# Adding two columns on VectorE ahead of one bfloat16 product with ones

## The chip, the core and the metric

The kernel runs on one core of a Trainium2 chip. A core has five engines that run their own lists of instructions in order and meet at semaphores: TensorE (PE in the profile; its weight loads are shown apart as PEld), VectorE (DVE), ScalarE (ACT), GpSimd (POOL) and SyncE (SP), which issues most of the transfers. The metric is the device time of one execution in microseconds, as the median of several runs.

## The reference

A transformer block over 2048 tokens of width 1024: a mixer of four HGRN2 heads and four retention heads in both directions, with a context of 256 tokens as initial state, and then a feed-forward part with a gated convolution. Cut to the parts that use the weights which matter here:

```python
hx = _rmsnorm(x, norm1_g[layer]) * (1.0 + sc1) + sh1
feats_x = _mixer_features(hx, w_in[layer], lb, (rows, cols))
...
x = x + g1 * (mix_x.astype(x.dtype) @ w_out[layer])
hx2 = _rmsnorm(x, norm2_g[layer]) * (1.0 + sc2) + sh2
gate, up = jnp.split(hx2 @ w_up_l, 2, axis=-1)
x = x + g2 * ((silu(conv(gate)) * up) @ w_down_l)
return _rmsnorm(x, final_g)
```

## The kernel before

All large products are float32 products made of float16 parts. A weight block is scaled by a power of two, split into a float16 and a float16 remainder, and multiplied in three products (`mm3`, lines 81 to 86). On top of that the projections use a seven-product block scheme: two weight tiles of 128 columns become a pair, from which seven combinations are made (`pair_blocks`, lines 638 to 646).

**The scale.** It comes from the sum of squares of the whole weight tile. ACT squares the tile, [128, 1024], and accumulates along the row, which leaves one float32 number in each of 128 partitions, a column of `ssq` (line 687 for the heads, `w_in`; line 1477 for the up projection, `w_up`). A pair of tiles gives two columns. `allsum` (lines 102 to 108) adds them over the partitions and hands the total to all of them: it multiplies a 128x128 matrix of ones (`onesq`, a view of one column with step 0) with each column, and lets the products add up in PSUM. DVE reads the total in `pow2` (lines 88 to 100), which makes the scale and its inverse by operations on exponent bits; `scales` (lines 648 to 660) adds the negative scale and the factor by which results are divided. With the scale known, ACT and DVE make the float16 parts of the weights (lines 643 and 644).

**Who calls it.** `head_weights` prepares the weights of the eight heads, always ahead of their use: per head a pair `z` and a pair `vg` (the last head has `v` and `g` as single tiles), and for the first four heads a single `q`. That gives 15 sums of two columns and 6 of one. `up_weights` is called 22 times, twice for each of the 11 blocks of the up projection, always with two columns; there, 16 small bfloat16 products (line 1482, `col`) with a column of bfloat16 ones, `onesb`, run just ahead of `allsum`. `out_weights`, `mixed_pairs` and `modulation` call it with one column, 13 times. So 37 sums have two columns and 19 have one.

**What sets the order.** The program is written as operations on tiles. A planner lays them out at build time with a simulated clock: for each engine it takes, among the instructions whose inputs are there, the one written earliest, and so it can issue an instruction well ahead of its place in the text. The order that comes out is fixed; on the chip an engine that has to wait holds up all that stands behind it in its list. Transfers of weights (`raw`, `wur`) are issued by SP. In the up projection four kinds of work share the time: PE multiplies the features by block j (lines 84 to 86), ACT and DVE take the results out of PSUM and do the convolution (lines 544 to 581), the weights of block j+1 are prepared, and the outputs of block j are split for the down projection (lines 1591 to 1593).

Of the kernel before, what the change touches and what calls it, by code (L numbers as in the profile page):

```python
# [11 lines left out]
BF16 = mybir.dt.bfloat16  # L12
# [3 lines left out]
ALU = mybir.AluOpType  # L16
PSUM = bass.MemoryType.PSUM

P = 128
# [27 lines left out]
def view(t, off, dims):  # L47
    return bass.AP(t.tensor, t.offset + off, [t.ap[0]] + dims)


class Kern:
# [49 lines left out]

    def allsum(self, cols, tag="tu"):

        o = self.ps(tag, [P, 1], "allsum")
        n = cols.shape[-1]
        for i in range(n):
            self.nc.tensor.matmul(o, self.onesq, cols[:, i:i + 1], start=i == 0, stop=i == n - 1, skip_group_check=True)
        return o

    def allmax(self, col, tag="tu"):  # L110
# [10 lines left out]
    def setup(self):  # L121

        nc, tc, ctx, I = self.nc, self.tc, self.ctx, self.I
# [19 lines left out]
        self.ones = cp.tile([P, 1], F32, name="ones")  # L143
        nc.gpsimd.memset(self.ones, 1.0)
        self.onesq = view(self.ones, 0, [[0, P]])
        self.dqx = cp.tile([P, 2], F32, name="dqx")
        self.xx = cp.tile([P, 1], F32, name="xx")
        self.sv = cp.tile([P, NV], F32, name="sv")
# [1291 lines left out]

    def ffn_setup(self):
        nc, cp = self.nc, self.cp
        self.onesb = cp.tile([P, 1], BF16, name="onesb")
        nc.vector.tensor_copy(self.onesb, self.ones)

        self.a2, self.c2 = (self.sv[:, V_BM + i * NF:V_BM + (i + 1) * NF] for i in range(2))
        t = self.slot_tile([P, 3 * NF], F32, "FG", "tabs")
        w = self.cw[:, :3 * NF]
        nc.vector.scalar_tensor_tensor(t, w, -1.0, w, ALU.mult, ALU.max)
        nc.vector.tensor_tensor(self.a2, t[:, :NF], t[:, NF:2 * NF], ALU.add)  # L1450
        nc.vector.tensor_tensor(self.a2, self.a2, t[:, 2 * NF:], ALU.add)
        nc.vector.tensor_tensor(self.a2, self.a2, self.a2, ALU.mult)
        nc.vector.tensor_scalar(self.a2, self.a2, self.xx, 2.0, ALU.mult, ALU.mult)
        c = self.cw[:, 3 * NF:]
        nc.vector.scalar_tensor_tensor(self.c2, c, 2.0, c, ALU.mult, ALU.mult)

        m = self.modT[:, 1]
        self.sas, self.ias = m[:, :NJ], m[:, NJ:2 * NJ]
        self.wq = m[:, 2 * NJ:4 * NJ], self.sv[:, :2 * NJ]
        self.W = {}  # L1460
        self.rows = {}
# [374 lines left out]
```

## Time and profile before

| what | value |
|---|---|
| median of 3 runs | 2742.63 us (2736.52 to 2743.33) |
| profiled execution | 2745.74 us |
| its span, first to last instruction | 2743.7 us |
| mean granted clock of TensorE | 0.967 |
| instructions | 56410 |

In the stretches of the span: the head weights and the first feature blocks up to about 210 us, the eight heads up to about 1230 us, the output projection up to about 1430 us, the up projection up to about 2290 us, and the down projection up to the end. Rows of the profile give the line of the kernel, the engine, the operation, what it writes and reads (`allsum<-ssqw,ones`), the shape, and how often. A timeline row begins with the start in us from the span's start and the duration; in brackets stands the idle time of the engine ahead of it, with the instruction that ended it. A group's row gives busy us and the mean ns of one. A float32 product shows as two records, each with a weight load of its own. The duration of a PE record contains the passage through the array, which overlaps with the next one's, so the start of the next record says how long PE was held. ACT's accumulated sum is read out by a second, short record (ACTIVATION_READ_ACCUMULATOR).

### The profile page before, as it was taken

Reading aid. Unit: us, or ns where it says so; the run is one execution under the profiler, and the core shown is the slowest. Engines: PE = TensorE matmul, PEld = TensorE weight load, DVE = VectorE, ACT = ScalarE, POOL = GpSimd, SP = SyncE. Lnnn points to the kernel's source line nnn. Section 1 sums busy time; section 2 is a strip of 40 time slices with the busy share of each in tenths; the row PEclk is TensorE's granted clock in tenths of the full one; section 3 lists DMA queues with packets and bytes.
Section 4 is the critical chain, followed back from the end, with each engine's and each line's share of the span. In section 5 each row is a group of like instructions: output and inputs, shape, how many; then the busy total and the mean of one; then the engine's idle time right before and its main releaser. Section 6 shows DMA issues by size and latency. Waiting matters only on the chain.

```text
span 2743.7 us, 56410 instructions
## 1 busy us (share of the span) xinstructions
PE 2562.4 (93%) x22829; PEld 1692.0 (62%) x22829; DVE 1835.8 (67%) x3569; ACT 1343.5 (49%) x2902; POOL 773.9 (28%) x905
## 2 busy tenths in 40 slices
PE   5789998999998989898999899999999999999998
PEld 2678887889888888787445344444444444444443
DVE  4998676775856666547464888778877777423553
ACT  5776456564544434336354665555555554411220
POOL 3742111220312132121244344344434433000101
PEclk7899999999999999999999999999999999999999
DMA  8224333343447766666532132333233234734552
GB/s 294 102 86 155 123 103 121 101 129 109 148 159 224 227 212 204 215 181 219 194 110 78 50 123 100 112 115 101 99 115 103 98 110 161 272 144 169 207 192 100
DMA packets 216693, 402.37 MB, mean 147 GB/s; under 512 B 16623, under 2 KB 98771, under 8 KB 211824
## 3 DMA queue, kind: packets, MB, share of 16 engines
q1 hardware_dynamic: 203808, 373.42, 40.1%
q10 hardware_dynamic: 12320, 25.18, 3.1%
q8 instruction: 178, 2.92, 0.4%
q14 instruction: 83, 0.68, 0.1%
q0 software_dynamic: 304, 0.17, 0.0%
HBM read 298.57 MB, written 91.75 MB: 142 GB/s over the span
## 4 chain that ended last, share of the span: by engine, by line
PE 63%; DVE 17%; DMA 7%; issue 6%; ACT 4%; POOL 3%; ACTq 0%; DVEq 0%; SPq 0%; POOLq 0%
PE pa L84 7%; PE pa L85 7%; PE pa L86 7%; PE pd L84 5%; PE pd L86 5%; PE pd L85 5%; PE pc L84 3%; PE pc L85 3%; PE pc L86 3%; PE pb L84 2%; PE pb L86 2%; PE pb L85 2%; PE opp L85 2%; PE opp L84 2%; PE opp L86 2%
## 5 line engine op out<-in xcount | busy, mean ns | idle before, releaser
L84 PE MATMUL pa<-feat,w 128*128 128x512 f16 x704 | 267.7, 380 | 8.6 <-ACT ta L544 8.0
L85 PE MATMUL pa<-feat,w 128*128 128x512 f16 x704 | 267.3, 380 | 1.1 <-DVE feat L1367 1.1
L86 PE MATMUL pa<-feat,w 128*128 128x512 f16 x704 | 263.9, 380 | 0.0
L85 PE MATMUL pd<-wd,actl 128*128 128x512 f16 x616 | 233.3, 379 | 0.0
L86 PE MATMUL pd<-wd,actl 128*128 128x512 f16 x616 | 233.3, 379 | 0.0
L84 PE MATMUL pd<-wd,actl 128*128 128x512 f16 x616 | 232.6, 379 | 0.1
L85 PEld LDWEIGHTS <-w 128*128 128x128 f16 x1232 | 120.8, 98 | 152.7 <-issue 12.9
L86 PEld LDWEIGHTS <-w 128*128 128x128 f16 x1232 | 121.4, 99 | 149.1 <-DVE w L644 2.9
L84 PEld LDWEIGHTS <-w 128*128 128x128 f16 x1232 | 121.7, 99 | 140.8 <-issue 1.6
L85 PEld LDWEIGHTS <-hx 128*128 128x128 f16 x1824 | 184.6, 101 | 11.7 <-issue 9.7
L86 PEld LDWEIGHTS <-hx 128*128 128x128 f16 x1824 | 184.6, 101 | 3.0 <-issue 1.9
L84 PEld LDWEIGHTS <-hx 128*128 128x128 f16 x1824 | 184.6, 101 | 2.4
L1592 DVE SCALAR_TENSOR_TENSOR st<-act,modT,st 128x512 f16<-128x512 f32 x154 | 142.9, 957 | 31.6 <-ACT st L1591 30.7
L84 PE MATMUL pa<-w_vg,hx 128*128 128x128 f16 x800 | 148.2, 224 | 5.5 <-DVE cb L578 4.6
L86 PE MATMUL pa<-w_vg,hx 128*128 128x128 f16 x800 | 148.2, 225 | 0.0
L85 PE MATMUL pa<-w_vg,hx 128*128 128x128 f16 x800 | 148.2, 224 | 0.0
L1591 ACT ACTIVATE st<-act,modT 128x512 f16<-128x512 f32 x154 | 107.5, 718 | 80.9 <-DVE act L1581 29.3
L86 PE MATMUL pc<-feat,w 128*128 128x512 f16 x352 | 134.1, 381 | 2.4 <-DVE w L644 2.4
L84 PE MATMUL pc<-feat,w 128*128 128x512 f16 x352 | 133.9, 380 | 2.3 <-ACT feat L1366 1.3
L85 PE MATMUL pc<-feat,w 128*128 128x512 f16 x352 | 133.9, 380 | 0.0
L84 PE MATMUL pa<-hx,w_z 128*128 128x256 f16 x464 | 128.7, 277 | 4.6 <-DVE K L586 2.1
L85 PEld LDWEIGHTS <-w_z 128*128 128x128 f16 x1072 | 108.7, 101 | 34.9 <-issue 23.0
(550 smaller groups left out, 7576.4 us busy)
## 6 DMA issues: line engine op xcount, KB each, us to landing
hx<-hxd SPq DMA_DIRECT2D x212, 512.0 KB, 5.0
actd<-st SPq DMA_DIRECT2D x154, 256.0 KB, 2.0
actl<-actd SPq DMA_DIRECT2D x28, 1024.0 KB, 5.1
wur<-in_w_up_dram SPq DMA_DIRECT2D x44, 512.0 KB, 4.1
raw<-in_w_in_dram SPq DMA_DIRECT2D x36, 512.0 KB, 4.3
wm<-in_w_mod_dram SPq DMA_DIRECT2D x64, 256.0 KB, 4.7
hxd<-hx SPq DMA_DIRECT2D x28, 512.0 KB, 3.4
wdb<-in_w_down_dram SPq DMA_DIRECT2D x44, 256.0 KB, 4.0
```

The source lines that it names most:

```text
L84: mm(ps, lhs(0), rhs(0), start=start, stop=False, skip_group_check=True)
L85: mm(ps, lhs(0), rhs(1), start=False, stop=False, skip_group_check=True)
L86: mm(ps, lhs(1), rhs(0), start=False, stop=stop, skip_group_check=True)
L1591: nc.scalar.activation(p[:, 0], v, AF.Copy, scale=s)
L1592: nc.vector.scalar_tensor_tensor(p[:, 1], v, s, p[:, 0], ALU.mult, ALU.subtract)
```

## The change

`allsum` with two columns now adds them on VectorE first, into a bfloat16 column `both` (two buffers), and makes one product with bfloat16 ones. With one column it does what it did: one float32 product. The bfloat16 column of ones `onesb`, so far made in `ffn_setup` by a conversion of the float32 column, is filled by a memset in `setup`. The total is thus rounded to bfloat16 per partition ahead of the sum over the partitions.

```diff
     def allsum(self, cols, tag="tu"):
 
+
         o = self.ps(tag, [P, 1], "allsum")
-        n = cols.shape[-1]
-        for i in range(n):
-            self.nc.tensor.matmul(o, self.onesq, cols[:, i:i + 1], start=i == 0, stop=i == n - 1, skip_group_check=True)
+        ones = self.onesq
+        if cols.shape[-1] == 2:
+            both = self.wp.tile([P, 1], BF16, tag="both", bufs=2, name="both")
+            self.nc.vector.tensor_tensor(both, cols[:, 0:1], cols[:, 1:2], ALU.add)
+            cols, ones = both, view(self.onesb, 0, [[0, P]])
+        self.nc.tensor.matmul(o, ones, cols, start=True, stop=True, skip_group_check=True)
         return o
...
         self.onesq = view(self.ones, 0, [[0, P]])
+        self.onesb = cp.tile([P, 1], BF16, name="onesb")
+        nc.vector.memset(self.onesb, 1.0)
...
     def ffn_setup(self):
         nc, cp = self.nc, self.cp
-        self.onesb = cp.tile([P, 1], BF16, name="onesb")
-        nc.vector.tensor_copy(self.onesb, self.ones)
```

## The prediction

> **What bounds the kernel now.** I read the page's busy shares and chain first, then the busy times by stretch, then every place where the changed sum runs.
>
> ```profile
> PE 2562.4 (93%) x22829; PEld 1692.0 (62%) x22829; DVE 1835.8 (67%) x3569; ACT 1343.5 (49%) x2902; POOL 773.9 (28%) x905
> ...
> PE 63%; DVE 17%; DMA 7%; issue 6%; ACT 4%; POOL 3%; ACTq 0%; DVEq 0%; SPq 0%; POOLq 0%
> ```
>
> TensorE (PE) is busy 93% of the span and carries 63% of the chain that ended last. A share of 93% is an average, so the stretches come next (columns: stretch, its length, then busy us and instructions of each engine in the order PE, PEld, DVE, ACT, POOL).
>
> ```profile
> 60.00:210.00 150.00, 118.46 (x1602) 101.27 (x1602) 137.82 (x295) 110.36 (x287) 87.70 (x115) 0.87 0.30 111
> 210.00:1230.00 1020.00, 936.27 (x13407) 858.52 (x13405) 674.55 (x1444) 504.10 (x1255) 208.22 (x241) 0.96 0.50 161
> ...
> 1640.00:2290.00 650.00, 648.44 (x3276) 301.81 (x3274) 521.44 (x892) 375.97 (x657) 263.64 (x175) 1.00 0.32 107
> 1430.00:1640.00 210.00, 196.67 (x1004) 94.35 (x1003) 156.95 (x264) 120.71 (x222) 94.25 (x105) 0.98 0.23 80
> ```
>
> Three regimes. From 60 to 210 us VectorE (DVE) is the fullest engine, 137.82 of 150 us. From 210 to 1230 us (heads 0 to 7) PE is busy 936.27 of 1020 us, so 83.7 us of idle time lie there. From 1640 to 2290 us (the up projection) PE idles 1.6 us in 650: whatever PE no longer issues there shortens the run one for one.
>
> **What the sum costs on PE today.** Each of the 37 two-column sums is four PE records, two per float32 column.
>
> ```profile
> L107 PE MATMUL allsum<-ssqw,ones x160: 169/250/373, 38.5 to 2272.9; 128*128 128x1 f32 x160
> ```
>
> 160 is 37 x 4 plus 6 one-column sums x 2. The 250 ns are no price: matmuls overlap, so I take start to start (the timeline of PE). First the last sum of the up projection, then two of the heads.
>
> ```profile
> 2272.43 0.29 PE L1482 MATMUL col<-onesb,w 128*128 128x1 bf16 x6
> 2272.59 0.58 PE L107 MATMUL allsum<-ssqw,ones 128*128 128x1 f32 x4
> 2273.03 0.38 PE L84 MATMUL pc<-feat,w 128*128 128x512 f16 x1
> ```
>
> ```profile
> 357.14 0.50 PE L107 MATMUL allsum<-ssqw,ones 128*128 128x1 f32 x4
> 357.51 0.27 PE L84 MATMUL pb<-hx,w_q 128*128 128x256 f16 x1
> ...
> 575.08 0.33 PE L107 MATMUL allsum<-ssqw,ones 128*128 128x1 f32 x2
> 575.28 0.36 PE L900 MATMUL o<-Sf,qf 128*128 128x128 f32 x1
> ```
>
> In the up projection the four hold PE from 2272.59 to 2273.03: **0.44 us**. In the heads, four together hold it 0.37 us, and where the planner put the two columns apart, 0.20 us per column. The replacement is one bfloat16 product with a 128x128 weight load and one moving column. That form stands just ahead: six L1482 products in 2272.43 to 2272.59, weight loads included, **0.027 us** each.
>
> Two rules of the Trainium skill would give other sums. "FP8 and Floating Point Precision", section TensorE Precision Notes, says true float32 takes four passes through the array; at 0.027 us a pass a pair would cost 0.22 us, and the 37 would save an estimated 7 us. The trace disagrees: a pair holds PE 0.44 us. "TensorE: Matmul & The Clock Gate", section LDWEIGHTS, gives a load of 128 columns as P/1.2, 107 ns, which would make the new product four times as dear and the saving an estimated 3 us smaller. The trace disagrees here too: the six loads and products came 27 ns apart.
>
> **The change, part by part.** (1) *PE, up projection.* 22 sums lie from 1430 to 2290 us. Each loses 0.44 - 0.027 = 0.41 us: 9.1 us. 17 of them lie in the stretch where PE never idles: 7.0 us, all of it on the path. Five lie from 1430 to 1640 us, where PE idles 13.3 us; of their 2.1 us I count 1.6.
>
> (2) *PE, heads.* 13 sums lie from 210 to 1230 us: five as four together, 5 x 0.37 = 1.9 us, eight in two halves, 8 x 0.40 = 3.2 us. Less 13 x 0.027 us this is 4.7 us of PE time. PE is 92% busy here, but its gaps are chains through DVE and ScalarE (ACT), some of which start at a DMA and absorb what PE saves. I take two thirds, 3.1 us; the bounds are 0 and 4.7. The two sums of head 0 stand before 210 us, where PE is not the bound: nothing.
>
> (3) *DVE, 37 adds.* The nearest form, a 128x1 add of two float32 columns:
>
> ```profile
> L1499 DVE TENSOR_TENSOR q<-q 128x1 f32<-128x1 f32 x11 | 1.7, 157 | 0.0
> ```
>
> 37 x 0.157 = 5.8 us of DVE. From 210 us on it is hidden behind PE: in the fullest stretch DVE works 521.44 of 650 us, and 17 adds are 2.7 us. If the cover were gone, all 5.8 us. One or two adds fall into the stretch from 60 to 210 us, where DVE is the bound: 0.2 us on the path.
>
> (4) *The wait.* The PE product waited for ACT's squares; now it waits for DVE, and DVE for the squares. In twelve of the 22 up sums there is ample time: the square was read out at 2247.85, its sum started at 2272.59. The other ten are tight (the first row is of the ample case, the next two of a tight one; timeline of ACT, then of DVE and PE).
>
> ```profile
> 2247.66 0.19 ACT L1477 ACTIVATION_READ_ACCUMULATOR w<-wur 128x1 f32 x1
> ...
> 2219.90 1.06 ACT L1477 ACTIVATE w<-wur 128x1024 bf16<-128x1024 f32 x1
> 2220.86 0.19 ACT L1477 ACTIVATION_READ_ACCUMULATOR w<-wur 128x1 f32 x1
> ```
>
> ```profile
> 2220.03 0.69 DVE L578 TENSOR_TENSOR ta<-pc,ta 128x512 f32<-128x512 f32 x1 [2.63 <-ACT ta L544]
> 2222.26 0.75 DVE L1561 SCALAR_TENSOR_TENSOR act<-ta,taps,act 128x511 f32<-128x511 f32 x1 [1.55 <-ACT act L1556]
> 2222.93 0.21 DVE L1567 SCALAR_TENSOR_TENSOR act<-edge,taps,act 128x1 f32<-128x1 f32 x1
> 2223.06 0.74 DVE L1562 SCALAR_TENSOR_TENSOR act<-ta,taps,act 128x511 f32<-128x511 f32 x1
> ...
> 2222.96 0.58 PE L107 MATMUL allsum<-ssqw,ones 128*128 128x1 f32 x4
> ```
>
> The squares are complete at 2221.05 and PE wants the sum at 2222.96; the add needs 0.16 us, and DVE stands idle for 1.55 us before L1561. In that hole it is done by about 2221.3. What queues behind it on DVE is L1561, which waits for ACT anyway. So I cost the wait at 0. Issued behind the three DVE rows it would delay PE by about 1 us: rival C. For the other sums, and those of the heads, the planner can move a ready instruction forward, as it did with the cast of the ones:
>
> ```profile
> L1444 DVE CAST onesb<-ones x1: 98/98/98, 1.0 to 1.0; 128x1 bf16<-128x1 f32 x1
> ```
>
> (5) *The ones.* That cast, written in the third stage, already ran at 1.0 us. A memset in its place, written in the setup, costs and saves nothing within 0.1 us. The two columns of `both` can hold up an add only until the second-last product has been read: nothing. No DMA is added or moved.
>
> **The sum.** 7.0 + 1.6 + 3.1 - 0.2 = 11.5 us less. The profiled execution took 2745.7 us (span 2743.7), so it becomes 2734.2. That execution lies 3.1 us above the median of the three runs, 2742.6; against the median the forecast is **2731 us**, 0.42% less. Below 0.3%, 8.2 us, a measurement of this kernel can't tell a change from none (its three runs lie 6.8 us apart).
>
> **Rivals.**
>
> *A, the heads give nothing* (2734): their 83.7 us of idle take up the 4.7 us. For: of the waits on the way some end at a DMA. Against: PE is busy 92%. Left is 7.0 + 1.6 us, 8.6, at the edge of what can be measured.
>
> *B, the ones are not cheap* (2734): a weight load that reads one column 128 times might take the pitch of one float32 record, 0.11 us (0.44/4). Then 35 sums save 0.085 us less each, 3.0 us. For: no row shows such a load in bfloat16. Against: two float32 loads of that one column took 0.30 us, two of a full matrix the same.
>
> ```profile
> 575.03 0.30 PEld L107 LDWEIGHTS allsum<-ssqw,ones 128*128 128x128 f32 x2
> 575.25 0.30 PEld L900 LDWEIGHTS o<-Sf,qf 128*128 128x128 f32 x2
> ```
>
> Cheaper ends than 0.027 us are worth below 1 us. By the LDWEIGHTS rule of the Trainium skill ("TensorE: Matmul & The Clock Gate") this rival would be the forecast; the 27 ns of the traced loads speak against it.
>
> *C, PE waits for the add in the tight places* (2741): if the add is issued behind the three DVE rows shown, it ends at about 2223.96 and PE waits 1.0 us. Ten such places take back 10 us of the 11.5. For: DVE is 80% busy there. Against: the hole of 1.55 us.
>
> *D, the planner's new order costs the heads something* (2742): one product fewer and one add more shift every later choice. If PE's idle time in the heads grows by an eighth, 10.5 us, the gain is gone; a better order could as well give some microseconds.
>
> *E, slower: DVE is held by late weights* (2762).
>
> ```profile
>   DMA raw<-in_w_in_dram: 29.5, 17
> ...
>   DMA wur<-in_w_up_dram: 32.5, 31
> ```
>
> These rows say how long ACT idled ahead of the squares, for `raw` (L687) and for `wur` (L1477): 62 us in all. Today only ACT is held. An add issued directly behind the square makes DVE wait as long, and with it the evacuations for which PE waits. About half, 31 us, lies ahead of the second square, which the add needs; passed on to PE in full it makes 31 - 11.5 = 19.5 us more. It decides the sign once PE is made to wait over 11.5 us. For: both engines run their lists in order. Against: DVE has other work in its list ahead of the add, and such a delay of ACT costs PE little today, as its 1.6 us of idle in 650 show.
>
> **How the numbers follow.** The forecast 0.52; A 0.11; B 0.05; C 0.10; D 0.11; E 0.11. A and B lie at the bound and count half as faster. Faster: 0.52 + 0.08 = 0.60; slower: E, 0.11; same: the rest, 0.29. For the range: all 13.8 us of (1) and (2) on the path give 2729, and a planner's order that by luck gives 4 us more, with a median run as low as the lowest of the three, 6 us, some 2719. Upward it takes in A, B, C and D and the spread of the runs above D: 2746. Left out are E and a little of the low end.
>
> **What would show it.** In the changed profile the two-column sums are 37 bfloat16 products and float32 records of `ssqw` fall from 160 to 12; PE's count falls by 111 to about 22718, DVE's grows by 37 to about 3606, and PE's busy time falls by some 14 us. From such a sum to the next product's start it is 0.03 us, not 0.44 (0.11 is B). Rows of PE waiting for the add, `both`, above 2 us in all would be C; DVE waiting for L687 or L1477 above 10 us would be E. The stretch of the up projection shortens by about 9 us; if the heads shorten by 0 it is A, if they grow it is D. I am wrong in the mechanism if PE's work falls by 14 us and the idle time of the up projection takes it back.

## The result, and the profile after

The changed kernel takes **2761.5 us** (median of 4 runs, 2756.0 to 2762.7) against 2743.0 for the kernel before (4 runs, 2736.5 to 2744.8): ratio **1.0065**, 95% interval 1.0051 to 1.0079. It is slower by 18 us where 12 us less were forecast.

What the change says it does, it does. The page's busy shares and the sum's own groups, after:

```profile
PE 2556.0 (93%) x22718; PEld 1678.2 (61%) x22718; DVE 1831.5 (66%) x3606; ACT 1342.5 (49%) x2903; POOL 777.2 (28%) x905
```

```profile
L111 PE MATMUL allsum<-both,onesb x37: 163/164/167, 38.7 to 2290.2; 128*128 128x1 bf16 x37
...
L111 PE MATMUL allsum<-ssqw,ones x12: 168/250/373, 44.5 to 1155.5; 128*128 128x1 f32 x12
```

```profile
2290.08 0.29 PE L1486 MATMUL col<-onesb,w 128*128 128x1 bf16 x6
2290.24 0.16 PE L111 MATMUL allsum<-both,onesb 128*128 128x1 bf16 x1
2290.26 0.38 PE L84 MATMUL pa<-feat,w 128*128 128x512 f16 x1
```

PE's records fell by 111 to 22718, and from the sum to the next product it is 0.02 us (the last rows, of PE's timeline) where it was 0.44. The work is gone. PE's busy time, though, fell by 6.4 us and not by the 14 that were expected: the mean granted clock of TensorE was 0.962 to 0.963 in the four runs, against 0.967 in the profiled run of the kernel before. The question is where the run got longer. I cut both spans at the same instructions: the first product `ub<-V,KTt`, the first `opp`, the first `pa<-feat,w`, the first `pd`. That gives five stages: the start, the heads, the output projection, the up projection and the down projection. Busy times by stretch, the kernel before:

```profile
0.00:183.40 183.40, 129.24 (x1324) 96.53 (x1324) 136.69 (x318) 119.87 (x301) 94.21 (x129) 0.80 0.50 180
183.40:1304.60 1121.20, 1021.25 (x14576) 937.44 (x14575) 755.53 (x1660) 568.93 (x1414) 237.90 (x288) 0.96 0.50 161
...
1492.90:2333.60 840.70, 825.81 (x4153) 384.34 (x4152) 674.51 (x1155) 486.11 (x853) 334.89 (x229) 0.99 0.32 108
```

And the changed kernel:

```profile
0.00:189.70 189.70, 129.79 (x1318) 95.87 (x1319) 137.60 (x320) 120.30 (x301) 92.68 (x129) 0.79 0.48 174
189.70:1331.50 1141.80, 1022.34 (x14537) 934.56 (x14536) 747.68 (x1673) 570.86 (x1415) 243.45 (x288) 0.96 0.49 158
...
1519.00:2350.90 831.90, 818.53 (x4091) 375.25 (x4090) 678.72 (x1177) 482.86 (x853) 335.02 (x229) 0.99 0.32 109
```

The up projection became 8.8 us shorter. The start became 6.3 us longer and the heads 20.6 us longer; the two other stages stayed within 1 us. In the heads PE was busy as long as before (1022.3 against 1021.3 us) and idle for 19.5 us more.

The first suspect is the new add. Its group on DVE, with the idle time ahead of it and what ended that:

```profile
L109 DVE TENSOR_TENSOR both<-ssqw 128x1 bf16<-128x1 f32 x37 | 14.8, 400 | 66.6 <-ACT w L1481 40.1 <-ACT w_z L693 16.4 <-ACT w_vg L693 10.1
```

DVE did stand in front of the adds for 66.6 us, 26.5 of them in the heads (L693). The figure is close to the loss, which makes it tempting. But 40.1 us lie in the up projection, the stage that won. The second suspect is the order: PE's list differs from that of before from 84 us on. Two theories follow, **HELD** (the wait of DVE is the loss) and **ORDER** (the new order is).

### The profile page after: what moved, and what is told of

It reads as the page before. It is cut to its first block, busy times and chain, and to the rows that moved or that the text cites. A ratio compares the mean times of both kernels' runs of the same rounds, so it can differ in the third digit from the quotient of the medians.

```text
span 2760.9 us, 56237 instructions
## 1 busy us (share of the span) xinstructions
PE 2556.0 (93%) x22718; PEld 1678.2 (61%) x22718; DVE 1831.5 (66%) x3606; ACT 1342.5 (49%) x2903; POOL 777.2 (28%) x905
## 4 chain that ended last, share of the span: by engine, by line
PE 49%; DVE 6%; DMA 5%; issue 4%; POOL 2%; ACT 1%; ACTq 0%; DVEq 0%; POOLq 0%; SPq 0%
PE pa L84 5%; PE pa L85 5%; PE pa L86 5%; PE pd L85 5%; PE pd L86 5%; PE pd L84 5%; PE pc L84 3%; PE pc L85 3%; PE pc L86 3%; DMA Q<-K 2%; PE opp L84 2%; PE opp L85 2%; PE opp L86 2%; PE pb L84 1%; PE pb L86 1%
## 5 line engine op out<-in xcount | busy, mean ns | idle before, releaser
L85 PEld LDWEIGHTS <-hx 128*128 128x128 f16 x1824 | 181.0, 99 | 25.0 <-issue 22.9
L86 PEld LDWEIGHTS <-hx 128*128 128x128 f16 x1824 | 181.8, 100 | 1.9 <-issue 1.1
L84 PEld LDWEIGHTS <-hx 128*128 128x128 f16 x1824 | 180.8, 99 | 2.1
L84 PE MATMUL pa<-w_vg,hx 128*128 128x128 f16 x800 | 147.2, 224 | 16.4 <-DVE cb L584 13.8
```

What stands on the lines that cost most here:

```text
L84: mm(ps, lhs(0), rhs(0), start=start, stop=False, skip_group_check=True)
L85: mm(ps, lhs(0), rhs(1), start=False, stop=False, skip_group_check=True)
L86: mm(ps, lhs(1), rhs(0), start=False, stop=stop, skip_group_check=True)
```

## The experiments

Each ratio is to the kernel before on the same chip. Where the lists of two programs are compared, the sums themselves are left out. The stages of all runs stand in a table at the end of this section. They are of one profiled run each, and this run can lie some microseconds from the median.

**e1, the new sum in the up projection only.**

```diff
-        if cols.shape[-1] == 2:
+        n = cols.shape[-1]
+        if n == 2 and tag == "sc":
             both = self.wp.tile([P, 1], BF16, tag="both", bufs=2, name="both")
             self.nc.vector.tensor_tensor(both, cols[:, 0:1], cols[:, 1:2], ALU.add)
-            cols, ones = both, view(self.onesb, 0, [[0, P]])
-        self.nc.tensor.matmul(o, ones, cols, start=True, stop=True, skip_group_check=True)
+            self.nc.tensor.matmul(o, view(self.onesb, 0, [[0, P]]), both, start=True, stop=True, skip_group_check=True)
+            return o
+        for i in range(n):
+            self.nc.tensor.matmul(o, self.onesq, cols[:, i:i + 1], start=i == 0, stop=i == n - 1, skip_group_check=True)
```

> The new sum in the up projection only; the heads keep their four float32 products, and with them the planner's order of before up to about 1400 us. Two theories for the loss: ORDER (the planner's changed order costs the heads about 26 us, the waits cost nothing) and HELD (DVE stands in its list behind an add whose weights come late, about 26 us of idle time ahead of `both` in the heads). Both expect here the heads unchanged and the up projection 9 us shorter: about 2734 us, ratio 0.9967. If it is 2743 or more, the up projection is where something is lost, and both are wrong.

Measured: 2737.5 us, ratio 0.9977 (0.9964 to 0.9989). The gain of the up projection stands by itself, and the loss lies ahead of it. DVE stood 43.1 us in front of these adds, and the up projection became shorter all the same.

**e2, the new sum in the heads only** (`tag == "tu"` in the same edit).

> The new sum in the heads only; the up projection keeps its four float32 products. Both theories expect the heads 26 us longer and nothing back: about 2769 us, ratio 1.0095. Near 2743 would say that the loss needs both parts together.

Measured: 2764.2 us, ratio 1.0076 (1.0059 to 1.0093). The heads' sums alone bring the loss. It is a little smaller than expected, about 21 us. Up to the end of the heads the lists of PE, DVE, ACT and GpSimd are those of the changed kernel in every place; the profiled run, the fastest of four, was 16.4 us late there, that of the changed kernel 26.9.

**e3, the add on GpSimd.**

```diff
-            self.nc.vector.tensor_tensor(both, cols[:, 0:1], cols[:, 1:2], ALU.add)
+            self.nc.gpsimd.tensor_tensor(both, cols[:, 0:1], cols[:, 1:2], ALU.add)
```

> The whole change, but the add on GpSimd, so that DVE waits for no square; the planned order of PE is that of the changed kernel in 97% of its places. HELD: the 26 us of the heads come back, about 2735 us, ratio 0.997. ORDER: it stays as slow as the changed kernel, 2755 to 2765 us, ratio 1.0045 to 1.008. In between: each has a part.

Measured: 2739.4 us, ratio 0.9978 (0.9965 to 0.9991). Almost everything that was lost came back, and ORDER's band, 2755 to 2765 us, was missed. That looked like a proof of HELD. It wasn't one: the edit takes the wait away, and also changes some 4% of the places of PE's list.

**e7, the wait alone in nearly the order of before**: the four float32 products stay, the add on DVE is made, nobody reads it.

```diff
+        if n == 2:
+            both = self.wp.tile([P, 1], F32, tag="both", bufs=2, name="both")
+            self.nc.vector.tensor_tensor(both, cols[:, 0:1], cols[:, 1:2], ALU.add)
         for i in range(n):
```

> The kernel before with its four float32 products, and beside them the add on DVE of the two columns, whose result nobody reads: the wait alone, in a planned order that is that of before in 94% of PE's places. HELD: DVE idles ahead of `both` for 20 us or more in the heads and the run takes 2760 to 2770 us, ratio 1.006 to 1.01. ORDER: 2740 to 2747 us, ratio 0.999 to 1.0015.

Measured: 2748.5 us, ratio 1.0012 (0.9999 to 1.0025). DVE idled 17.2 us ahead of the adds of the heads, a little less than HELD asked for, and some 3 us reached the end. This speaks against HELD.

**e5, the add on DVE, but not moved up.**

```diff
+            last = getattr(self, "last", None)
+            with self.tc.issue_after(last.ins) if last else ExitStack():
-            self.nc.vector.tensor_tensor(both, cols[:, 0:1], cols[:, 1:2], ALU.add)
+                self.nc.vector.tensor_tensor(both, cols[:, 0:1], cols[:, 1:2], ALU.add)
```

> The whole change with the add on DVE, but issued behind the last evacuation written before it, so that the planner can no longer move it up to the square; PE's planned order keeps 93% of the changed kernel's places. HELD: DVE's idle time ahead of `both` in the heads falls from 26 us to below 8, and the run to about 2742 us, ratio 0.997 to 1.001. ORDER: idle time falls too, and the run stays at 2755 to 2765, ratio above 1.004.

Measured: 2791.8 us, ratio 1.0184 (1.0165 to 1.0203), far outside both. DVE's wait in the heads did fall, to 5.2 us, and yet the run first lost as much as the changed kernel: at 620 us of the kernel before, the same PE instructions started 16 us late in both, at 860 us 17 us late in both. So that much can be lost without DVE standing in front of the adds. At the end of the heads e5 was 16.2 us late, like e2 (16.4), and the changed kernel 26.9. The rest of e5's loss is a new wait in the up projection, which grew from 840.7 to 874.8 us. Who waited for whom, e5, in that stage (total us, times, longest):

```profile
PE col L1488 <- ACT w L1483: 30.2, 9, 4.3
```

In the order that came out of this edit, PE's small products stand in front of squares that ACT has not yet made. Holding back one small instruction per sum made this stage 34 us longer than before.

**e6, no add at all**: the squares are accumulated into bfloat16 columns, two bfloat16 products. Shown against the kernel before; the ones are made in the setup as in the change.

```diff
+        ones = view(self.onesb, 0, [[0, P]]) if n == 2 else self.onesq
         for i in range(n):
-            self.nc.tensor.matmul(o, self.onesq, cols[:, i:i + 1], start=i == 0, stop=i == n - 1, skip_group_check=True)
+            self.nc.tensor.matmul(o, ones, cols[:, i:i + 1], start=i == 0, stop=i == n - 1, skip_group_check=True)
...
-                ssq = self.kp.tile([P, n], F32, tag=f"ssqw{n}", bufs=2, name="ssqw")
+                ssq = self.kp.tile([P, n], BF16 if n == 2 else F32, tag=f"ssqw{n}", bufs=2, name="ssqw")
...
-        ssq = kp.tile([P, 2], F32, tag="ssqw2", bufs=2, name="ssqw")
+        ssq = kp.tile([P, 2], BF16, tag="ssqw2", bufs=2, name="ssqw")
```

> No add at all: the squares are accumulated into bfloat16 columns, and two bfloat16 products with ones take the place of four float32 ones. Nothing on DVE waits for a square. PE's work falls by about 13 us. HELD: 2735 to 2742 us, ratio 0.996 to 1.0. ORDER: the changed order of the heads still costs some 20 us, 2750 us or more, ratio above 1.003.

Measured: 2741.7 us, ratio 1.0000 (0.9985 to 1.0014). It lies in HELD's band of time, as e3 did, but the saving of the up projection (6.0 us in its profile, which is of its slowest run) is used up: the start is 189.7 us long, as in the changed kernel. A kernel without any such add or wait loses those 6 us too.

**e9 and e10, head 0 as before**; e10 has the adds on GpSimd besides.

```diff
-    def allsum(self, cols, tag="tu"):
+    def allsum(self, cols, tag="tu", old=False):
...
+        if old and cols.shape[-1] == 2:
+            for i in range(2):
+                self.nc.tensor.matmul(o, ones, cols[:, i:i + 1], start=i == 0, stop=i == 1, skip_group_check=True)
+            return o
...
-                s, neg, dq = self.scales(self.allsum(ssq), self.dqx[:, 0:1] if h else None, "dq" + nm)
+                s, neg, dq = self.scales(self.allsum(ssq, old=h == 0), self.dqx[:, 0:1] if h else None, "dq" + nm)
```

> The whole change except for the two sums of head 0, which keep four float32 products; up to about 250 us the planned order is that of before. In the changed kernel and in the one with the add on GpSimd, the same 8 us are lost by 260 us, where no add has held DVE yet. If that is the changed order of the first feature blocks, they are gone: about 2753 us, ratio 1.0035, and the held adds of the later heads still cost their 18 us. If the early loss has another cause it stays: 2761 us, 1.0065.

> Both mended: head 0 with its four float32 products, all other pairs with the add on GpSimd. If the two causes add up, 8 us below the run with the add on GpSimd alone: about 2731 us, ratio 0.995, faster than both kernels. If the early loss isn't the order of head 0, 2739 us, 0.998.

Measured: e9 2747.5 us, ratio 1.0014 (1.0000 to 1.0028); e10 2737.0 us, ratio 0.9976 (0.9960 to 0.9992). e9 is faster than either expectation. Two sums out of 37, of which nothing was to be saved, carry most of the loss: with them left alone the kernel is 14 us faster than the changed one. The start is 185.4 us long again. DVE still stands 24.8 us in front of the heads' adds in e9, about as long as in the changed kernel, and still most of the loss is gone. In the heads the lists of PE, DVE, ACT and GpSimd are those of the changed kernel in every place, sums included; the heads took 1127.4 us in e9, 1132.3 in e2 and 1141.8 in the changed kernel. So neither this order of the heads nor DVE's waits in it fix the time of the heads. e10 did not add up: it equals e3. With the adds on GpSimd the same two sums thus cost next to nothing, though the start is longer there too (187.9 us in e3, 184.4 in e10).

What the two sums do in the start can be seen on DVE, changed kernel first, then the kernel before:

```profile
139.90 0.29 DVE L584 TENSOR_TENSOR cb<-pa,cb 128x128 f32<-128x128 f32 x1 [5.37 <-PE pa L86]
```

```profile
134.18 0.29 DVE L578 TENSOR_TENSOR cb<-pa,cb 128x128 f32<-128x128 f32 x1 [1.06 <-ACT cb L544]
```

In the new order DVE, the fullest engine of the start, stands 5.37 us in front of a product of PE, where it waited 1.06 us before. A wait of 5.1 to 5.7 us in this place is in the start of all eight kernels with a new head 0, with the add on DVE, on GpSimd or without one, and in none of the eight others. PE's products ahead of it ran at half the clock in the changed kernel: the granted clock was 0.50 from 134.5 to 138 us and 1.00 from there to 140 us. How much of the wait is the order and how much the clock was not separated.

**e11 and e14, the wait alone in an order that doesn't move.** On top of e10 and of e3, in all head sums that are new there, DVE makes the same add once more, unread. All three lists of PE, DVE and ACT keep the order of e10 and e3 in every place.

```diff
-            both = self.wp.tile([P, 1], BF16, tag="both", bufs=2, name="both")
+            both = self.wp.tile([P, 2], BF16, tag="both", bufs=2, name="both")
+            pair, both = both, both[:, 0:1]
             self.nc.gpsimd.tensor_tensor(both, cols[:, 0:1], cols[:, 1:2], ALU.add)
+            if tag == "tu":
+                self.nc.vector.tensor_tensor(pair[:, 1:2], cols[:, 0:1], cols[:, 1:2], ALU.add)
```

> The kernel of e10 (head 0 as before, adds on GpSimd) with a second add of the same two columns on DVE in heads 1 to 7, whose result nobody reads. Every engine's planned list is that of e10, place by place, apart from the 13 adds: the wait on DVE alone. HELD: DVE idles some 20 us ahead of these adds, and about half reaches the end: 8 to 12 us above e10, about 2747 us, ratio 1.0005 to 1.002. ORDER: as e10, 2737 us, ratio 0.9976.

> The same wait on top of e3 (adds on GpSimd, head 0 changed too), whose planned lists it keeps place by place, and whose lists of DVE and ACT agree with the changed kernel's in 99%. HELD: it becomes as slow as the changed kernel, 2755 to 2762 us, ratio 1.004 to 1.0065. ORDER: as e3, 2739 us, ratio 0.998. Between the two, each has a part: what is above e3 is the wait, what is left to the changed kernel is the order.

Measured: e11 2736.9 us, ratio 0.9970 (0.9959 to 0.9981); e14 2743.2 us, ratio 0.9997 (0.9985 to 1.0008). DVE's waits in e11:

```profile
L116 DVE TENSOR_TENSOR both<-ssqw x13: 146/161/164, 222.5 to 1029.5; 128x1 bf16<-128x1 f32 x13
its engine sat idle before it (us, times) until:
  ACT w_z L700: 12.0, 6
  ACT w_vg L700: 10.0, 3
```

22 us of waiting, and the run is as fast as without (0.9976). On e3's order 21.2 us of waiting cost about 5 us by the medians (0.9997 against 0.9978, whose intervals overlap); the heads of the two profiled runs are equally long (1124.7 and 1124.5 us). HELD falls as the main cause: the wait is worth 0 to 5 us by the medians, 10 at most by the intervals. From e14 to the changed kernel, with the same sums and nearly the same waits on DVE, some 19 us remain, and these two differ in order, and in the engine that feeds PE. PE's own waiting for DVE's adds is not it: in the changed kernel that is 0.8 us in all, in two places.

**e4, adds of constants.** The kernel before with an add of constants in every sum of two; the lists of before stay in every place.

```diff
+            self.nc.vector.tensor_tensor(both, self.ones, self.ones, ALU.add)
```

> The kernel before, and in all 37 sums an add on DVE that reads constants and whose result nobody reads: the adds without any wait, in exactly the planned lists of before. Both theories: 5.8 us more of DVE work, hidden: 2743 us, ratio 0.999 to 1.001. Above 1.002 the adds themselves would cost something.

Measured: 2742.3 us, ratio 0.9995 (0.9984 to 1.0006). This shows less than was expected of it, by where the adds ran:

```profile
L108 DVE TENSOR_TENSOR both<-ones x37: 96/155/161, 1.0 to 5.4; 128x1 f32<-128x1 f32 x37
```

As they wait for nothing, the planner put all 37 into the first 5.4 us. That adds spread over the heads are hidden is shown by e11, whose 13 adds stand between 222.5 and 1029.5 us. Of use is e4 as a repetition of the lists of before.

**e15, head 0 only**: the opposite of e9.

```diff
-        if old and cols.shape[-1] == 2:
+        if not old and cols.shape[-1] == 2:
```

> The new sum only in the two pairs of head 0, at 38 and 75 us; the other 35 keep their float32 products. Nothing is saved there, and no add holds DVE up. Theory ORDER: the planner takes another order from 100 us on, the first stage (before the first of the heads' state products) becomes 5 to 6 us longer as in the changed kernel, and the heads may follow: 2747 to 2755 us, ratio 1.001 to 1.004. If the loss of the first stage came from the adds or products themselves, it would have been there in e9's heads too, and here the run would be as before, 2743 us, ratio 0.999 to 1.001.

Measured: 2755.7 us, ratio **1.0044** (1.0030 to 1.0058), just above ORDER's band. Two sums, of which no add stood idle for a square, cost 13 us. The stages of e15, by a profiled run that is its slowest, 4 us above the median:

```profile
0.00:188.60 188.60, 130.70 (x1317) 96.19 (x1318) 137.69 (x320) 120.35 (x300) 92.53 (x129) 0.79 0.49 175
188.60:1311.10 1122.50, 1019.50 (x14576) 936.78 (x14576) 749.93 (x1660) 569.27 (x1415) 240.08 (x288) 0.96 0.49 161
...
1499.10:2347.90 848.80, 827.74 (x4153) 384.37 (x4152) 672.83 (x1156) 483.93 (x853) 332.95 (x229) 0.99 0.32 107
```

5.2 us in the start, 1.3 in the heads, and 8.1 in the up projection, where the same number of PE instructions runs as before (4153) and PE is idle 21 us instead of 15. In the heads the lists of PE, DVE, ACT and GpSimd are those of before; in the up projection 3592 of PE's 4068 records are in the places of before. So an early change of order comes back in a stage 1400 us later, whose list differs too; by one profile each, the size of it is uncertain by the 4 us named.

**e16 and e17, the squares moved back.** In the changed kernel the squares of the next head's weights are issued on ACT behind the last gate evacuation written ahead of them; e17 leaves head 0 as before besides.

```diff
+                    held = getattr(self, "gated", None)
+                    with self.tc.issue_after(held.ins) if held else ExitStack():
-                    nc.scalar.activation(junk, r.rearrange("p k t -> p (k t)"), AF.Square, scale=4.0 if n == 2 else 1.0,
-                                         accum_out=ssq[:, i:i + 1])
+                        nc.scalar.activation(junk, r.rearrange("p k t -> p (k t)"), AF.Square, scale=4.0 if n == 2 else 1.0,
+                                             accum_out=ssq[:, i:i + 1])
...
-            nc.scalar.activation(FG[:, d, half * n // 2:(half + 1) * n // 2], self.whole(c, s), AF.Sigmoid, scale=dq)
+            self.gated = nc.scalar.activation(FG[:, d, half * n // 2:(half + 1) * n // 2], self.whole(c, s), AF.Sigmoid, scale=dq)
```

Why there: the timeline of the changed kernel around the second square of one pair of weight tiles (`w_z`), ACT first, then DVE, then PE.

```profile
617.31 1.06 ACT L693 ACTIVATE w_z<-raw 128x1024 f16<-128x1024 f32 x1 [3.41 <-DMA raw<-in_w_in_dram]
618.27 0.19 ACT L693 ACTIVATION_READ_ACCUMULATOR w_z<-raw 128x1 f32 x1
618.37 0.60 ACT L878 COPY qf<-Q 128x512 f32<-128x512 f32 x1
618.88 0.50 ACT L725 ACTIVATE FG<-ct,dq 128x256 f32<-128x256 f32 x1
```

```profile
618.49 0.16 DVE L109 TENSOR_TENSOR both<-ssqw 128x1 bf16<-128x1 f32 x1 [4.95 <-ACT w_z L693]
619.41 0.55 DVE L728 TENSOR_SCALAR FG<-FG,omlb,lb 128x512 f32<-128x512 f32 x1 [0.76 <-ACT FG L725]
619.87 0.34 DVE L889 SCALAR_TENSOR_TENSOR KTt<-Sb,T,ub 128x128 f32<-128x128 f32 x1
```

```profile
620.27 0.79 PE L887 MATMUL op<-KTt,Q 128*128 128x128 f32 x2 [3.48 <-DVE KTt L889]
```

ACT stands 3.41 us in front of a square whose weights have not landed, with the gate evacuation (L725) behind it. DVE stands 4.95 us in front of the add, then 0.76 us more for that evacuation, and PE 3.48 us for what DVE then makes. In the kernel before, around the same pair on ACT:

```profile
598.98 1.06 ACT L687 ACTIVATE w_z<-raw 128x1024 f16<-128x1024 f32 x1 [1.96 <-DMA raw<-in_w_in_dram]
...
601.92 1.06 ACT L687 ACTIVATE w_z<-raw 128x1024 f16<-128x1024 f32 x1 [0.15 <-DMA raw<-in_w_in_dram]
```

The first square of the pair waited 1.96 us for its weights and the second 0.15 us, and by PE's timeline from 597 to 607 us PE was idle once, for 0.63 us. Added up over the heads, from the start of each such wait of ACT to 2.5 us behind its square, PE was idle about 12 us in the changed kernel, 5 in the kernel before, and 10 in e5, where an add held DVE for 5.2 us only.

> The whole change, and the squares of the next head's weights issued on ACT behind the last gate evacuation that is written ahead of them, so that ACT, and with it the add on DVE, stands less in front of weights that have not landed. PE keeps 98% of the changed kernel's places. If the place of the squares in the planned order is what costs the heads (ACT waiting for raw weights with gate evacuations behind it, PE idle for 12 us around these waits against 5 before): that idle time falls below 4 us, and the run is 8 to 12 us faster than the changed kernel, 2749 to 2754 us, ratio 1.002 to 1.004. If it isn't: as the changed kernel, 2761 us, 1.0065.

> The same with head 0's two sums left as before. If both places of the order count and add up: the first stage as before, no waits in the heads, and the up projection 9 us shorter: 2732 to 2738 us, ratio 0.996 to 0.998, faster than both kernels, with the add on DVE. If only head 0 counts: as e9, 2747 us, 1.0014.

Measured: e16 2752.4 us, ratio 1.0029 (1.0018 to 1.0040), 9 us better than the changed kernel, as ORDER expected; PE's idle time around the waits fell to about 6 us, less than expected. DVE's wait in the heads fell too, from 26.5 to 20.3 us, so e16 alone does not tell the two apart. e17 2744.3 us, ratio 1.0004 (0.9992 to 1.0016): better than e9 by less than the runs can tell, and not the 2732 to 2738 that were expected. The two places of the order don't add up here either.

The stages of the runs side by side, in us, from the same cuts:

| run | start | heads | up projection | ratio |
|---|---|---|---|---|
| before | 183.4 | 1121.2 | 840.7 | 1 |
| changed | 189.7 | 1141.8 | 831.9 | 1.0065 |
| e1, up projection only | 184.6 | 1113.5 | 835.8 | 0.9977 |
| e2, heads only | 188.8 | 1132.3 | 839.4 | 1.0076 |
| e4, adds of constants | 184.9 | 1118.8 | 839.4 | 0.9995 |
| e7, wait alone | 183.1 | 1125.2 | 840.9 | 1.0012 |
| e3, add on GpSimd | 187.9 | 1124.5 | 832.1 | 0.9978 |
| e5, add held back | 189.2 | 1131.6 | 874.8 | 1.0184 |
| e6, no add | 189.7 | 1127.6 | 834.8 | 1.0000 |
| e14, e3 with the wait | 188.0 | 1124.7 | 833.4 | 0.9997 |
| e9, head 0 as before | 185.4 | 1127.4 | 834.9 | 1.0014 |
| e10, both | 184.4 | 1117.8 | 833.2 | 0.9976 |
| e11, e10 with the wait | 183.2 | 1116.3 | 835.7 | 0.9970 |
| e15, head 0 only | 188.6 | 1122.5 | 848.8 | 1.0044 |
| e16, squares moved back | 187.7 | 1133.9 | 833.0 | 1.0029 |
| e17, e16 and head 0 as before | 184.4 | 1124.4 | 837.7 | 1.0004 |

Before, e1 and e4 have the same lists in the heads, and their heads took 1113.5 to 1121.2 us: in one profile the heads alone are uncertain by some 8 us. This spread is mostly busy time at another clock. The heads of e1, to be set beside the second row of the kernel before above:

```profile
184.60:1298.10 1113.50, 1013.10 (x14576) 929.84 (x14576) 752.81 (x1660) 569.23 (x1415) 240.21 (x288) 0.97 0.50 162
```

The same 14576 records kept PE busy 8.2 us less at a granted clock of 0.97 than at 0.96, and its idle time is 100.4 us against 100.0. So idle time compares better than length: PE idled 100 to 103 us in the heads of the four runs with the order of before there (before, e1, e4, e15), 119.5 in the changed kernel, 114.5 in e2, 106.7 in e9, 108.1 in e3 and 106.0 in e14. The start is sharp: wherever head 0 is new it takes 187.7 to 189.7 us, elsewhere 183.1 to 185.4.

## Why the prediction was wrong

**Where it held.** Part (1): 8.6 us were forecast for the up projection, 8.8 were measured, which is close partly by luck, as e1 gained 6 us by its ratio (4.9 in this stage of its profile). The new product was priced at 0.027 us and took 0.02 us, so rival B, the ones that are not cheap, did not occur. Part (3): the adds are hidden (e1 in the up projection, e11 in the heads), though they were mis-sized: 14.8 us instead of 5.8, as nine of the 37 took longer (told below). Part (4), the tight places of the up projection: PE waited for no add there (its 0.8 us lie ahead of a sum of head 0 and one of head 4), so rival C did not occur; DVE idled 40 us ahead of the adds of this stage and it gained all the same.

**The step that failed** is the sum itself, which takes the order of everything else as given. Part (2) set the two sums of head 0 at "nothing", as PE is not the bound there. They turned the order: e15 puts 13 us on them alone, and e9 wins 14 back by leaving them. Part (2) also expected between 0 and 4.7 us less in the heads and took 3.1; it came out as 20.6 us more (11.0 in e2, with the same lists), with 6.3 us more in the start, for which part (3) had 0.2. Nothing in the terms allowed for that: the order's effect stood in the sum as zero. It was named, as rival D, with an eighth of PE's idle time in the heads, 10.5 us, as its price and a chance of 0.11. D's sign came true, PE's idle time in the heads grew by 19.5 us (14.5 in e2); the price was too small, and it was taken as something that ends near no change. With 10.5 us the rival lay within the range, with the 16 to 27 us that were lost up to the end of the heads (e2, changed kernel) it ends slower. The start, where DVE is the fullest engine, was not in D at all. The granted clock was not in the sum either: PE's work fell as forecast and its busy time by less than half of that.

**Rival E** saw the idle time: 62 us were named ahead of the squares, and DVE then stood idle for 66.6 us ahead of the adds. Its sign, more than 10 us of such waiting, came true, and its time, 2762 us, is the measured one by luck. It was wrong that the wait would be passed on. In orders that stay fixed, 22 us of it cost nothing (e11) and 21 us cost about 5 (e14). E had late weights right as a part of the story, and was wrong in the engine: what the rows show there is that ACT's squares stand ahead of gate evacuations, in the order that e16 changed for a gain of 9 us.

**What stays open.** About 4 to 6 us lie in the start and go with head 0's order; there the wait is found. For the heads the cause is not shown in full. The start's new order with the old heads cost them 1.3 us (e15), the new heads with the old start 6.2 us (e9), both together 11.0 and 20.6 us (e2 and the changed kernel), and the spread of one profile's heads is some 8 to 10 us. e16 moves 9 us of the whole with the place of the squares; the wait on DVE has some 0 to 5. A lower granted clock goes along with the loss in the changed kernel (0.963 against 0.967) but not in e15 (0.967 to 0.970); whether it is cause or effect was not tested. That the two sums of head 0 cost 13 to 14 us with the adds on DVE (e15, e9) and next to nothing with them on GpSimd (e3 against e10), and that e17 does not add up from its parts, shows that these shares are not independent. Why the planner's order of before is among the short ones was not tried.

## What to carry to other kernels

Where a planner lays out the instructions, an edit has two prices: that of its own instructions, which can be read from rows of the profile, and that of the order which comes out, which can't, and which here took some 16 to 27 us from the start and the heads against a gain of 5 to 9 us in the up projection. So put the edit only where the bound engine has no idle time and thus a row's price is the whole price (the up projection alone: 0.9977), and leave the places where nothing is to be saved as they were. Before an idle time in the changed profile is called the cause, let it be made again in an order that doesn't move: an unread instruction that waits in the same place (e11) cost nothing here, though its idle time was longer than the loss of the whole run. And where one profile is set beside another, let a run with the same lists say how far two profiles differ by themselves: the heads of the changed kernel and of e2 differ by 9.6 us.

## What the runs showed of the hardware that was not expected

Nine of the 37 adds took longer than the others, all of them beside a GpSimd instruction: eight took 1.22 to 1.23 us and one 0.58 us. DVE and GpSimd in the changed kernel:

```profile
2264.93 1.80 POOL L497 TENSOR_TENSOR act<-act 128x512 f32<-128x512 f32 x1
2265.53 1.23 DVE L109 TENSOR_TENSOR both<-ssqw 128x1 bf16<-128x1 f32 x1
```

An add of one element per partition took 1.23 us instead of 0.16 and ended within 0.03 us of the GpSimd instruction that was running when it began. The same holds for the eight others of the nine; the 28 that are left began beside no running GpSimd instruction and took at most 0.164 us. The Trainium skill, "SBUF — State Buffer", section SBUF: two separate sides, says that a DVE instruction with two inputs in SBUF and a GpSimd instruction that reads SBUF take one pair of ports by turns, each for its whole length; these rows agree. The small size of such an instruction on DVE is thus no bound on its time where GpSimd works.
